# Eight column tiles of a modulation vector made by VectorE in one stage instead of by TensorE in a later one

## The chip, the cores and the metric

One core of a Trainium2 chip runs the whole program. The metric is the device time of one execution in microseconds (us). Below, PE or TensorE is the matrix engine, DVE the vector engine, ACT or ScalarE the activation engine, POOL or GpSimd the fourth compute engine, and SP an engine that here only issues DMAs.

## What is computed

The model has two layers. Each layer has a mixer (input projection, four branches, gated sum, output projection) and a feed-forward (SwiGLU), both with adaptive normalisation. The three groups of 128 tokens (one of a prompt, two of a sample) share all weights. The scale, shift and gate vectors of the normalisation, called modulation, come from a small product with 2 condition vectors, one for each token kind:

```python
def modulation(c_vec, w_mod, b_mod):
    m = (jax.nn.silu(c_vec) @ w_mod + b_mod)[:, None, :]
    return jnp.split(m, 6, axis=-1)
...
for l in range(DEPTH):
    sh_m, sc_m, gt_m, sh_f, sc_f, gt_f = modulation(c, w_mod[l], b_mod[l])
    x, _ = mixer_sublayer(x, sh_m, sc_m, gt_m, p, ctx)
    x = ffn_sublayer(x, sh_f, sc_f, gt_f, p)

def ffn_sublayer(x, shift, scale, gate, p):
    h = rms_norm(x, p['norm_ffn_pre']) * (1.0 + scale) + shift
    f = (jax.nn.silu(h @ p['ffn_w_gate']) * (h @ p['ffn_w_up'])) @ p['ffn_w_down']
    return x + gate * rms_norm(f, p['norm_ffn_post'])
```

A layer's modulation has 6 x 1024 = 6144 columns, 48 tiles of 128. Tiles 32 to 39 (columns 4096 to 5119) are `sc_f`, the scale of the feed-forward's normalisation; it is needed when that layer's mixer has ended.

## The kernel before

All activations are kept transposed, features on the partitions and the 384 tokens along the free axis. Every large weight is split by the kernel into a high and a low part: ACT copies a piece of the raw weight to `whi` (line 419), DVE or POOL subtracts it from the raw weight to give `wlo_` (line 421), and TensorE runs three products per 128 x 128 block (lines 686 to 688: high by high, high by low, low by high). A piece is 512 columns, that is four blocks or 12 products. `take_half` hands out a piece and has the pieces up to four ahead split, into four buffers of each kind (`HB = 4`). Which engine subtracts follows a count: `cnt["n"] % 4 < cnt["pool"]` sends it to POOL. `POOL_FFN = (3, 2)` makes that three of four pieces in the first feed-forward and two of four in the second.

Raw weights come in units of up to 1024 columns, in the order of a list (`layer_plan`), into three buffers. In the mixers ACT's queue issues them, in the feed-forwards SP's. The order of instructions on each engine is fixed when the program is built.

Modulation is made in two ways. In the mixers, `mod_step` follows a gate product (tiles 0 to 23 of 32 in each mixer): it takes one raw unit of `w_mod`, 128 rows by 1024 columns, and multiplies it with the condition vectors on TensorE (`mod_mm`, line 517, four 256-column products). After eight steps ACT copies the sum out (`mod_copy`), TensorE transposes it and DVE adds the bias (`mod_place`, lines 551 and 555). Each step also ends with a `yield`, at which `run` lets the two side programs of the mixer (the recurrent branch and the attention branches) move on; so the steps also set how those are interleaved.

In the feed-forwards, `mod_some` makes whole tiles of 128 output columns on DVE: for each tile a transposed 128 x 1024 weight `rawm` is loaded by SP (three buffers), and `mod_vector` runs two multiply-and-sum instructions on it, one for each condition vector (line 563). `VMOD` lists these tiles and `VMOD_IN` says which feed-forward makes them: 24 in the first, 8 in the second. `add_bias` adds the bias after each eight.

The feed-forward's first part is a loop over tiles m of 128 hidden columns. In each turn TensorE makes gate and up (two pieces each), and `hidden` combines them: ACT line 1763, DVE lines 1764 and 1765, ACT line 1767 (the high part), DVE line 1768 (the low part). Then `mod_some` works on the tiles loaded a turn earlier and issues the loads of the next. Here a turn is called a period; one with two tiles of modulation is a double. The second part multiplies with `ffn_w_down`.

Of the kernel before, what the change touches and what calls it, by code (L numbers as in the profile page):

```python
# [45 lines left out]
HOLD, HLAST = 2, 4  # L46
REST = (5, 6, 7, 7)

VMOD = [(0, m) for m in range(40, 48)] + [(1, m) for m in range(16)] + [(1, m) for m in range(40, 48)]
VMOD_IN = (range(0, 24), range(24, 32))  # L50
YORD = (0, 1, 2, 3, 5, 4, 6, 7)

Z_ORDER = ("vb", "k0", "r0", "va", "k1", "r1", "gq0", "gq1", "gk", "glo")
# [29 lines left out]
def _split_k(nk, width):  # L83
    per = max(1, 1024 // width)
    return [(k, min(per, nk - k)) for k in range(0, nk, per)]


def layer_plan(l):
    out = []

    def gemm(kind, what, nk, width):
        for k, n in _split_k(nk, width):
            out.append((kind, l, what, k, n, width))

    def z(name):
        gemm("z", name, KD, len(COLS[name]))

    def mod(ll, sg, i):
        out.append(("mod", ll, (sg, i // 8), i % 8, 1, 1024))

    for k in KORD:
        out.append(("wide_z", l, None, k, 1, 768))
    for n in Z_ORDER:
        z(n)
    tiles = [(b, m) for b in GATE_ORDER for m in range(8)]
    for i in range(len(tiles) + LAG):
        if i == 8:
            for n in ("cq0", "cq1", "ckv"):
                z(n)
        if i < len(tiles):  # L110
            z("gate%d_%d" % tiles[i])
            if i < 24:
                mod(l, 1 + i // 16, i % 16)
        if i >= LAG:
            b, m = tiles[i - LAG]
            if m % 2 == 1:
                out.append(("br", l, (b, m // 2), 0, 2, 256))
    for m in range(8):
        gemm("out", m, KD, 128)
    for k in KORD:  # L120
        out.append(("wide_f", l, None, k, 1, 768))
    for m in range(3, FM):
        gemm("gate", m, KD, 128)
        gemm("up", m, KD, 128)
    for m in range(8):
        gemm("down", m, FM, 128)
    return out
# [200 lines left out]
def build(tc, I, O):  # L328
# [191 lines left out]
    mod_late = []  # L520
# [259 lines left out]
    def mixer(l, x, xspill, hs, M, merged_of):  # L780
# [67 lines left out]
        def main():  # L848
            for n, q in zip(WIDE_Z, wide_ps):
                z_evac(n)(q)  # L850
            for n in Z_ORDER:
                if n in ("va", "vb"):
                    yield from gemm_tok(("z", l, n), hz, len(COLS[n]), va_evac if n == "va" else vb_evac)
                else:
                    yield from gemm(("z", l, n), hz, z_evac(n))
            tiles = [(b, m) for b in GATE_ORDER for m in range(8)]
            merged = None
            for i in range(len(tiles) + LAG):
                if i == 8:
                    for n in ("cq0", "cq1", "ckv"):  # L860
                        yield from gemm(("z", l, n), hz, z_evac(n))
                if i < len(tiles):
                    b, m = tiles[i]
                    yield from gemm(("z", l, "gate%d_%d" % (b, m)), hz, gate_evac(b, m))
                    if i < 24:
                        mod_step(l, 1 + i // 16, i % 16)
                        yield
                if i == 25 and mod_late:
                    mod_place(*mod_late.pop(), bk_mm())
                if i >= LAG and (i - LAG) % 2:  # L870
                    b, m1 = tiles[i - LAG]
                    yield lambda: b in ready
                    if merged is None:
                        merged = merged_of()
                        mref.append(merged)
                    hi, lo = take_half(next_unit(("br", l, (b, m1 // 2))))[0]
                    for m in (m1 - 1, m1):
                        ps = bk_mm()
                        for k in range(2):
                            o = (m % 2) * 256 + k * 128  # L880
                            xh, xl = brs[b, k][:, 0, :], brs[b, k][:, 1, :]
                            T.matmul(ps[:, :NT], hi[:, o:o + 128], xh, start=(k == 0), stop=False)  # L882
                            T.matmul(ps[:, :NT], hi[:, o:o + 128], xl, start=False, stop=False)  # L883
                            T.matmul(ps[:, :NT], lo[:, o:o + 128], xh, start=False, stop=(k == 1))  # L884
                            yield
                        gt = gates.pop((b, m))
                        if b == GATE_ORDER[0]:
                            V.scalar_tensor_tensor(merged[:, m, :], gt, 1.0, ps[:, :NT], op0=OP.add, op1=OP.mult)
                        else:
                            V.scalar_tensor_tensor(gt, gt, 1.0, ps[:, :NT], op0=OP.add, op1=OP.mult)  # L890
                            (G if m % 2 else V).tensor_add(merged[:, m, :], merged[:, m, :], gt)  # L891
                    if m1 == 7:
                        ready.add(("used", b))
# [814 lines left out]
    for l in range(L):  # L1708
# [18 lines left out]
        with tc.tile_pool(name=f"ffn{l}", bufs=1) as M:  # L1727
            if l + 1 < L:
                load_params(l + 1)
                scale_params(l + 1)  # L1730
                load_rest(l + 1)
            cb = M.tile([128, 2, D], F32, name="cb")
            dma(cb, bass.AP(tensor=csd.tensor, offset=csd.offset, ap=[[0, 128], [D, 2], [1, D]]))
            acc = M.tile([128, len(VMOD), 2], F32, name="acc")
            todo = list(VMOD_IN[l])

            def add_bias(t):

                (ml, m0), t0 = VMOD[t - 7], t - 7
                b = PAR[ml]["vec"][:, V_BMOD + m0:V_BMOD + m0 + 8, None]  # L1740
                V.tensor_add(mod_tile(ml)[:, m0:m0 + 8, :], acc[:, t0:t + 1, :], b.to_broadcast([128, 8, 2]))

            there = []

            def mod_some(n, behind):

                with tc.issue_after(behind.ins):
                    for t, raw in there:
                        junk = M.tile([128, D], F32, name="junk", tag="junk")
                        mod_vector(t, cb, acc, raw, junk)  # L1750
                        if t % 8 == 7:
                            add_bias(t)
                there.clear()
                for t in todo[:n]:
                    raw = M.tile([128, D], F32, name="rawm", tag="rawm", bufs=3)
                    dma(raw, I["wm1"][t])
                    there.append((t, raw))
                del todo[:n]
            hid = []

            def hidden(m, pg, pu):
                th = M.tile([128, NT], F32, name="th", tag="th", bufs=2)
                S.activation(th, pg[:, :NT], AF.Tanh, scale=0.5)
                V.scalar_tensor_tensor(th, th, 1.0, pg[:, :NT], op0=OP.add, op1=OP.mult)
                V.scalar_tensor_tensor(th, th, 0.5, pu[:, :NT], op0=OP.mult, op1=OP.mult)  # L1765
                h = M.tile([128, 2, NT], F32R, name=f"hid{m}", tag=f"hid{m}")
                S.activation(h[:, 0, :], th, AF.Copy)  # L1767
                last = V.tensor_sub(h[:, 1, :], th, h[:, 0, :].bitcast(F32))  # L1768
                hid.append((h[:, 0, :], h[:, 1, :]))
                return last  # L1770

            def ffn_main():
                got = list(wide_ps)
                cnt["pool"] = POOL_FFN[l]
                for m in range(3):
                    hidden(m, got[2 * m], got[2 * m + 1])
                hk = [hs[k] for k in range(KD)]
                for m in range(3, FM):
                    got = []
                    bk = (bk_at, bk_mm)[m % 2]  # L1780
                    yield from gemm(("gate", l, m), hk, got.append, bk=bk)
                    yield from gemm(("up", l, m), hk, got.append, bk=bk)
                    ins = hidden(m, *got)
                    mod_some(2 if m % 3 == 0 else 1, ins)

            drive(ffn_main())
            assert not todo and not there
            cnt["pool"] = POOL_FFN[l] - 1 if l == 0 else 1
            last = l + 1 == L
            mg, ps = out_gemm("down", l, hid, post_scale(l, 1), x, M, "z", ("sq0", "sq1", "sq2"), ("th",), not last)  # L1790
            if last:
                post_norm(x, mg, ps[0])
            else:
                hs, sx = bridge(x, mg, ps, sx, scales(l + 1, 0), shift(l + 1, 0), ("wide_z", l + 1, None))
# [27 lines left out]
```

## Time and profile before

| what | value |
|---|---|
| time, median of 3 runs | 1599.79 us (1592.71 to 1599.82) |
| the profiled execution | 1595.09 us, of which the traced span is 1593.3 us |
| PE busy | 1539.9 us (97%) |
| DVE busy | 973.9 us (61%) |
| ACT busy | 640.0 us (40%) |
| POOL busy | 460.7 us (29%) |
| line 517 in the two mixers | 384 records, 391 ns each |
| line 563 | 64 instructions, 1460 ns each |

Shares are averages over the span. A matmul counts as busy from its start to its modelled end, so consecutive ones overlap: two starts, not two durations, give the pace. One f32 matmul of line 517 shows as two records.

### The profile page before, as it was taken

The numbers are of one execution on the slowest core, as the hardware profiler recorded it, in microseconds if no ns is written. First come the engines' busy times: TensorE is split into PE (matmuls) and PEld (weight loads), VectorE is DVE, ScalarE is ACT, GpSimd is POOL, SyncE is SP. The second block draws the span as 40 slices with busy tenths as digits, with TensorE's granted clock in tenths as the row PEclk, the third lists the DMA queues.
The fourth block names the chain that finished last, engine by engine and source line by source line (L and its number), as shares of the span: only waits on it lengthen the run. The fifth ranks groups of instructions, "written<-read, shape, count | busy, mean of one in ns | idle before, by whom it ended". The sixth has DMA issues, their size and how long they took to land. (4 is left out here: it accounts for less than half of the span.)

```text
span 1593.3 us, 28472 instructions
## 1 busy us (share of the span) xinstructions
PE 1539.9 (97%) x11036; PEld 1394.9 (88%) x11036; DVE 973.9 (61%) x2165; ACT 640.0 (40%) x1364; POOL 460.7 (29%) x357
## 2 busy tenths in 40 slices
PE   8999999999999999999989999999999989999997
PEld 6988778777899999999989887876789889999997
DVE  5478458844558677863475774677554777844333
ACT  3454334432343544433345533434323435444331
POOL 2210002111226555544452100012012453433222
PEclk9999999999998999999999999999999989999999
DMA  8544343435542556644334542353354416544332
GB/s 330 196 130 136 97 130 110 137 94 150 165 159 77 188 197 213 213 154 130 113 110 130 150 132 79 110 144 110 95 156 131 160 54 213 181 132 130 119 125 77
DMA packets 106759, 225.32 MB, mean 141 GB/s; under 512 B 41280, under 2 KB 51584, under 8 KB 105728
## 3 DMA queue, kind: packets, MB, share of 16 engines
q1 hardware_dynamic: 76384, 124.99, 24.9%
q10 hardware_dynamic: 30240, 98.51, 19.3%
q8 instruction: 87, 1.43, 0.4%
q14 instruction: 48, 0.39, 0.1%
HBM read 214.38 MB, written 9.08 MB: 140 GB/s over the span
## 5 line engine op out<-in xcount | busy, mean ns | idle before, releaser
L419 ACT ACTIVATE whi<-raw 128x512 fp32r<-128x512 f32 (+2 forms) x580 | 345.9, 603 | 492.0 <-PE bank L687 265.2
L686 PE MATMUL bank<-hk,whi 128*128 128x384 f32 x1424 | 501.2, 352 | 1.5 <-DVE gate L890 0.9
L687 PE MATMUL bank<-hk,whi 128*128 128x384 f32 x1424 | 481.0, 338 | 1.9 <-DVE hk L1527 1.9
L686 PEld LDWEIGHTS bank<-hk,whi 128*128 128x128 f32 x1424 | 268.1, 188 | 26.7 <-issue 14.6
L687 PEld LDWEIGHTS bank<-hk,whi 128*128 128x128 f32 x1424 | 268.4, 188 | 6.6 <-DVE hk L1527 3.1
L686 PE MATMUL bank<-hid,whi 128*128 128x384 f32 x352 | 119.1, 338 | 0.0
L687 PE MATMUL bank<-hid,whi 128*128 128x384 f32 x352 | 118.9, 338 | 0.0
L563 DVE SCALAR_TENSOR_TENSOR junk<-rawm,cb 128x1024 f32<-128x1024 f32 x64 | 93.4, 1460 | 0.5
L710 PE MATMUL bank<-hk,whi 128*128 128x384 f32 x192 | 62.9, 341 | 6.1 <-DVE hk L618 5.6
L708 PE MATMUL bank<-hk,whi 128*128 128x384 f32 x192 | 65.5, 341 | 0.9 <-ACT hk L610 0.7
L687 PEld LDWEIGHTS bank<-hid,whi 128*128 128x128 f32 x352 | 66.1, 188 | 0.0
L686 PEld LDWEIGHTS bank<-hid,whi 128*128 128x128 f32 x352 | 66.1, 188 | 0.0
L891 POOL TENSOR_TENSOR merged<-merged,gate 128x384 f32<-128x384 f32 x24 | 29.3, 1221 | 111.8 <-DVE gate L890 98.4
L1564 POOL TENSOR_TENSOR acc<-acc,sqo 128x384 f32<-128x384 f32 x42 | 51.3, 1233 | 30.9 <-ACT sqo L1554 15.8
L1768 DVE TENSOR_TENSOR hid<-th,hid 128x384 fp32r<-128x384 f32 x44 | 42.7, 970 | 22.6 <-ACT hid L1767 22.6
L843 ACT ACTIVATE gate<-bank 128x384 f32<-128x384 f32 x64 | 31.1, 486 | 61.4 <-PE bank L688 49.9
L1765 DVE SCALAR_TENSOR_TENSOR th<-th,bank 128x384 f32<-128x384 f32 x44 | 24.3, 552 | 37.9 <-PE bank L688 37.4
L911 ACT ACTIVATE prob<-bank,tiny 128x384 f32<-128x384 f32 (+1 forms) x56 | 27.2, 485 | 47.5 <-DVE tiny L910 40.2
L1557 DVE TENSOR_SCALAR mg<-bank,Q 128x128 f32<-128x128 f32 x64 | 23.6, 408 | 32.7 <-ACT sqo L1554 31.5
L710 PEld LDWEIGHTS bank<-hk,whi 128*128 128x128 f32 x192 | 35.8, 188 | 8.4 <-DVE hk L618 6.6
L890 DVE SCALAR_TENSOR_TENSOR gate<-gate,bank 128x384 f32<-128x384 f32 x48 | 26.4, 550 | 22.1 <-PE bank L884 21.8
L708 PEld LDWEIGHTS bank<-hk,whi 128*128 128x128 f32 x192 | 36.5, 190 | 2.2 <-ACT hk L610 1.1
(2019 smaller groups left out, 3581.2 us busy)
## 6 DMA issues: line engine op xcount, KB each, us to landing
raw<-in_w ACTq DMA_DIRECT2D x150, 512.0 KB, 3.6
raw<-in_w SPq DMA_DIRECT2D x108, 512.0 KB, 3.5
rawm<-in_wm SPq DMA_DIRECT2D x32, 512.0 KB, 3.5
raw<-in_w SPq DMA_DIRECT2D x41, 384.0 KB, 3.0
wm<-in_wm SPq DMA_DIRECT2D x16, 512.0 KB, 7.6
raw<-in_w ACTq DMA_DIRECT2D x32, 256.0 KB, 2.6
raw<-in_w ACTq DMA_DIRECT2D x15, 384.0 KB, 3.6
bt<-in_bt SPq DMA_DIRECT2D x8, 256.0 KB, 4.2
```

Source lines behind the costliest of these rows:

```text
L419: last_split[:] = [S.activation(hi[:, :w], raws[i][:, sl], AF.Copy)]
L563: V.scalar_tensor_tensor(junk, raw, 1.0, cb[:, g, :], op0=OP.mult, op1=OP.mult, accum_out=acc[:, t, g:g + 1])
L686: T.matmul(ps[:, :n], wh, xh, start=(k == 0), stop=False)
L687: T.matmul(ps[:, :n], wh, xl, start=False, stop=False)
L708: T.matmul(o, wh, xh, start=(i == 0), stop=False)
L710: T.matmul(o, wh, xl, start=False, stop=(i == 7))
L843: S.activation(gates[b, m], ps[:, :NT], AF.Tanh, scale=0.5)
L890: V.scalar_tensor_tensor(gt, gt, 1.0, ps[:, :NT], op0=OP.add, op1=OP.mult)
L891: (G if m % 2 else V).tensor_add(merged[:, m, :], merged[:, m, :], gt)
L911: S.activation(e[:, :n], src, AF.Exp, bias=nb, scale=scale, accum_out=sm)
L1564: (V if i == 1 else G).tensor_add(a, a, b)
L1768: last = V.tensor_sub(h[:, 1, :], th, h[:, 0, :].bitcast(F32))
```

## The change

The eight steps of layer 1 that made tiles 32 to 39 leave the second mixer, and the eight tiles join the list of the first feed-forward, which makes 32 tiles now. The loads move with them: eight raw units of 512 KB leave ACT's queue in the second mixer, eight `rawm` loads of 512 KB join SP's queue in the first feed-forward. `mod_some` takes two tiles in every period instead of two, one, one; that also holds for the eight tiles of the second feed-forward.

```diff
--- before.py
+++ after.py
@@ -46,8 +46,9 @@
 HOLD, HLAST = 2, 4
 REST = (5, 6, 7, 7)
 
-VMOD = [(0, m) for m in range(40, 48)] + [(1, m) for m in range(16)] + [(1, m) for m in range(40, 48)]
-VMOD_IN = (range(0, 24), range(24, 32))
+VMOD = [(0, m) for m in range(40, 48)] + [(1, m) for m in (*range(16), *range(32, 40))] + [(1, m) for m in range(40, 48)]
+VMOD_IN = (range(0, 32), range(32, 40))
+MMOD = (24, 16)
 YORD = (0, 1, 2, 3, 5, 4, 6, 7)
 
 Z_ORDER = ("vb", "k0", "r0", "va", "k1", "r1", "gq0", "gq1", "gk", "glo")
@@ -109,7 +110,7 @@
                 z(n)
         if i < len(tiles):
             z("gate%d_%d" % tiles[i])
-            if i < 24:
+            if i < MMOD[l]:
                 mod(l, 1 + i // 16, i % 16)
         if i >= LAG:
             b, m = tiles[i - LAG]
@@ -862,10 +863,10 @@
                 if i < len(tiles):
                     b, m = tiles[i]
                     yield from gemm(("z", l, "gate%d_%d" % (b, m)), hz, gate_evac(b, m))
-                    if i < 24:
+                    if i < MMOD[l]:
                         mod_step(l, 1 + i // 16, i % 16)
                         yield
-                if i == 25 and mod_late:
+                if i == MMOD[l] + 1 and mod_late:
                     mod_place(*mod_late.pop(), bk_mm())
                 if i >= LAG and (i - LAG) % 2:
                     b, m1 = tiles[i - LAG]
@@ -1781,7 +1782,7 @@
                     yield from gemm(("gate", l, m), hk, got.append, bk=bk)
                     yield from gemm(("up", l, m), hk, got.append, bk=bk)
                     ins = hidden(m, *got)
-                    mod_some(2 if m % 3 == 0 else 1, ins)
+                    mod_some(2, ins)
 
             drive(ffn_main())
             assert not todo and not there
```

Line numbers in the changed kernel are one higher than before. On DVE, in the middle of the first feed-forward (`hid` is the hidden tile's low part, `th` its two steps, `junk` the modulation, `wlo_` a weight's low part), the program before reads, from one period's end over a double into a single:

```order
L1768 TENSOR_TENSOR hid_6831<-th,hid_6831 128x384
L563 SCALAR_TENSOR_TENSOR junk,acc<-rawm,cb 128x1024
L421 TENSOR_TENSOR wlo__6862<-raw,whi 128x512
L563 SCALAR_TENSOR_TENSOR junk,acc<-rawm,cb 128x1024 x2
L1764 SCALAR_TENSOR_TENSOR th<-th,bank 128x384
L563 SCALAR_TENSOR_TENSOR junk,acc<-rawm,cb 128x1024
L1765 SCALAR_TENSOR_TENSOR th<-th,bank 128x384
L1768 TENSOR_TENSOR hid_6916<-th,hid_6916 128x384
L563 SCALAR_TENSOR_TENSOR junk,acc<-rawm,cb 128x1024
L421 TENSOR_TENSOR wlo__6944<-raw,whi 128x512
L563 SCALAR_TENSOR_TENSOR junk,acc<-rawm,cb 128x1024
L1764 SCALAR_TENSOR_TENSOR th<-th,bank 128x384
```

The same place in the changed program, two periods:

```order
L1769 TENSOR_TENSOR hid_6764<-th,hid_6764 128x384
L564 SCALAR_TENSOR_TENSOR junk,acc<-rawm,cb 128x1024
L422 TENSOR_TENSOR wlo__6797<-raw,whi 128x512
L564 SCALAR_TENSOR_TENSOR junk,acc<-rawm,cb 128x1024 x2
L1765 SCALAR_TENSOR_TENSOR th<-th,bank 128x384
L564 SCALAR_TENSOR_TENSOR junk,acc<-rawm,cb 128x1024
L1766 SCALAR_TENSOR_TENSOR th<-th,bank 128x384
L1769 TENSOR_TENSOR hid_6851<-th,hid_6851 128x384
L564 SCALAR_TENSOR_TENSOR junk,acc<-rawm,cb 128x1024
L422 TENSOR_TENSOR wlo__6884<-raw,whi 128x512
L564 SCALAR_TENSOR_TENSOR junk,acc<-rawm,cb 128x1024 x2
L1765 SCALAR_TENSOR_TENSOR th<-th,bank 128x384
```

Every period is now a double: four modulation instructions stand between one `hid` and the next, three of them ahead of the first `th` step, and none of the periods has only two.

On DVE in the second feed-forward, where two weight pieces of four are DVE's, the program before reads, for its second and third period with modulation, one tile each:

```order
L1768 TENSOR_TENSOR hid_14741<-th,hid_14741 128x384
L563 SCALAR_TENSOR_TENSOR junk,acc<-rawm,cb 128x1024 x2
L421 TENSOR_TENSOR wlo__14786<-raw,whi 128x512
L1764 SCALAR_TENSOR_TENSOR th<-th,bank 128x384
L421 TENSOR_TENSOR wlo__14804<-raw,whi 128x512
L1765 SCALAR_TENSOR_TENSOR th<-th,bank 128x384
L1768 TENSOR_TENSOR hid_14823<-th,hid_14823 128x384
L563 SCALAR_TENSOR_TENSOR junk,acc<-rawm,cb 128x1024 x2
L421 TENSOR_TENSOR wlo__14870<-raw,whi 128x512
L1764 SCALAR_TENSOR_TENSOR th<-th,bank 128x384
```

and in the changed program:

```order
L1769 TENSOR_TENSOR hid_14729<-th,hid_14729 128x384
L564 SCALAR_TENSOR_TENSOR junk,acc<-rawm,cb 128x1024 x3
L422 TENSOR_TENSOR wlo__14779<-raw,whi 128x512
L564 SCALAR_TENSOR_TENSOR junk,acc<-rawm,cb 128x1024
L422 TENSOR_TENSOR wlo__14797<-raw,whi 128x512
L1765 SCALAR_TENSOR_TENSOR th<-th,bank 128x384
L1766 SCALAR_TENSOR_TENSOR th<-th,bank 128x384
L1769 TENSOR_TENSOR hid_14816<-th,hid_14816 128x384
L564 SCALAR_TENSOR_TENSOR junk,acc<-rawm,cb 128x1024 x3
L422 TENSOR_TENSOR wlo__14866<-raw,whi 128x512
L564 SCALAR_TENSOR_TENSOR junk,acc<-rawm,cb 128x1024
L422 TENSOR_TENSOR wlo__14884<-raw,whi 128x512
```

The doubles stand next to each other now, with both low parts behind the third and the fourth modulation instruction.

On TensorE in the second mixer, at one of the eight steps (`hk` is the normalised input, `brX` a branch's output), the program before reads:

```order
L687 MATMUL bank<-hk,whi 128x384
L688 MATMUL bank<-hk,wlo__12830 128x384
L517 MATMUL bank<-raw,cs 32x256 x4
L882 MATMUL bank<-brX,whi 128x384
L883 MATMUL bank<-brX,whi 128x384
L884 MATMUL bank<-brX,wlo__12910 128x384
```

and now:

```order
L688 MATMUL bank<-hk,whi 128x384
L689 MATMUL bank<-hk,wlo__12841 128x384
L883 MATMUL bank<-brX,whi 128x384
L884 MATMUL bank<-brX,whi 128x384
L885 MATMUL bank<-brX,wlo__12883 128x384
```

The step is gone and the branch product follows the gate product directly. Elsewhere between the steps the side programs' matmuls stand a few rows from where they stood.

## Rows read from the trace of the kernel before

**Rows 1.** All engines by windows, first feed-forward; busy PE PEld DVE ACT POOL, clock, DMA.

```profile
560.00:600.00 40.00, 40.00 (x232) 40.00 (x231) 31.97 (x48) 16.76 (x30) 22.46 (x14) 1.00 0.60 203
```

**Rows 2.** TensorE's timeline, second mixer: start, duration, line, operation; x8 are eight records.

```profile
1182.41 0.34 PE L688 MATMUL bank<-hk,wlo__13022 128*128 128x384 f32 x1
1182.68 0.64 PE L517 MATMUL bank<-raw,cs 128*32 128x256 f32 x8
1183.25 0.45 PE L882 MATMUL bank<-brX,whi 128*128 128x384 f32 x1
```

**Rows 3.** TensorE's timeline at the placing of the removed columns, second mixer.

```profile
1207.54 0.34 PE L688 MATMUL bank<-hk,wlo__13279 128*128 128x384 f32 x1
...
1208.37 0.44 PE L882 MATMUL bank<-brX,whi 128*128 128x384 f32 x1 [0.27 <-DVE MOD L555]
```

**Rows 4.** DVE's timeline, first feed-forward, a period with two tiles and the next.

```profile
610.09 0.55 DVE L1765 SCALAR_TENSOR_TENSOR th<-th,bank 128x384 f32<-128x384 f32 x1 [1.26 <-PE bank L688]
...
612.32 1.21 DVE L563 SCALAR_TENSOR_TENSOR junk<-rawm,cb 128x1024 f32<-128x1024 f32 x1
...
615.32 2.21 DVE L563 SCALAR_TENSOR_TENSOR junk<-rawm,cb 128x1024 f32<-128x1024 f32 x1
...
617.92 1.85 DVE L563 SCALAR_TENSOR_TENSOR junk<-rawm,cb 128x1024 f32<-128x1024 f32 x1
...
619.71 0.54 DVE L1765 SCALAR_TENSOR_TENSOR th<-th,bank 128x384 f32<-128x384 f32 x1
620.84 0.56 DVE L1768 TENSOR_TENSOR hid<-th,hid 128x384 fp32r<-128x384 f32 x1 [0.59 <-ACT hid L1767]
621.32 1.22 DVE L563 SCALAR_TENSOR_TENSOR junk<-rawm,cb 128x1024 f32<-128x1024 f32 x1
...
622.46 0.69 DVE L421 TENSOR_TENSOR wlo__6944<-raw,whi 128x512 fp32r<-128x512 f32 x1
...
626.73 0.56 DVE L1765 SCALAR_TENSOR_TENSOR th<-th,bank 128x384 f32<-128x384 f32 x1 [1.97 <-PE bank L688]
```

**Rows 5.** POOL's timeline in the same stretch.

```profile
608.59 1.30 POOL L421 TENSOR_TENSOR wlo__6812<-raw,whi 128x512 fp32r<-128x512 f32 x1 [0.47 <-ACT whi L419]
...
614.84 1.60 POOL L421 TENSOR_TENSOR wlo__6879<-raw,whi 128x512 fp32r<-128x512 f32 x1 [2.87 <-ACT whi L419]
...
619.00 1.94 POOL L421 TENSOR_TENSOR wlo__6926<-raw,whi 128x512 fp32r<-128x512 f32 x1 [0.31 <-ACT whi L419]
```

**Rows 6.** POOL's and DVE's timelines in the first output product.

```profile
478.41 1.07 POOL L1564 TENSOR_TENSOR acc<-acc,sqo 128x384 f32<-128x384 f32 x1 [2.89 <-ACT sqo L1560]
...
478.52 1.50 DVE L421 TENSOR_TENSOR wlo__5497<-raw,whi 128x512 fp32r<-128x512 f32 x1
```

**Rows 7.** TensorE's timeline: first use of two low parts that DVE made.

```profile
618.55 0.33 PE L688 MATMUL bank<-hk,wlo__6862 128*128 128x384 f32 x1
...
626.87 0.33 PE L688 MATMUL bank<-hk,wlo__6944 128*128 128x384 f32 x1
```

**Rows 8.** ScalarE's timeline, first feed-forward: the hidden tile's copy and the split behind it.

```profile
620.28 0.53 ACT L1767 ACTIVATE hid<-th 128x384 fp32r<-128x384 f32 x1 [1.36 <-DVE th L1765]
620.71 0.62 ACT L419 ACTIVATE whi<-raw 128x512 fp32r<-128x512 f32 x1
```

**Rows 9.** DVE's timeline, second feed-forward, a period with two tiles.

```profile
1344.64 0.56 DVE L1765 SCALAR_TENSOR_TENSOR th<-th,bank 128x384 f32<-128x384 f32 x1 [0.85 <-PE bank L688]
...
1351.54 0.69 DVE L421 TENSOR_TENSOR wlo__14704<-raw,whi 128x512 fp32r<-128x512 f32 x1
...
1354.54 0.55 DVE L1765 SCALAR_TENSOR_TENSOR th<-th,bank 128x384 f32<-128x384 f32 x1
```

**Rows 10.** TensorE's timeline there: first use of that low part.

```profile
1355.19 0.33 PE L688 MATMUL bank<-hk,wlo__14704 128*128 128x384 f32 x1
```

**Rows 11.** All engines by windows, two bridges; clock is the number behind POOL's.

```profile
520.00:525.00 5.00, 2.46 (x13) 1.82 (x12) 5.00 (x9) 2.24 (x5) 3.38 (x3) 1.00 0.28 79
...
805.00:810.00 5.00, 3.77 (x16) 3.80 (x17) 4.17 (x13) 1.75 (x4) 1.47 (x3) 0.52 0.00 0
```

## The prediction

> **What bounds the kernel now.** I read the busy shares first, then the windows of the two stages that the change touches, then the timelines of each engine there. In the first feed-forward TensorE is busy for all 40 us of a window while DVE is busy for 31.97 and POOL for 22.46 [rows 1], so by the shares TensorE sets the pace and DVE has a fifth to spare. The pace itself is the distance between the first uses of two low parts that stand at the same place of neighbouring periods: 626.87 - 618.55 = 8.32 us [rows 7]. That is 48 products at 0.173 us, without a gap.
>
> The timelines show why DVE's share misleads. A modulation instruction takes 1.21 us when POOL is idle, but 2.21 us and 1.85 us where POOL has asked during the one before it [rows 4, 5]. POOL's subtraction is longer too in those places, 1.60 and 1.94 us instead of 1.30 [rows 5]. So the two take turns: whoever has asked first works, the other stands still and still counts as busy. It needs no pause on DVE: in another stage POOL asked at 478.41, and DVE's next subtraction, from 478.52, took 1.50 us [rows 6] instead of 0.69 [rows 4]. The `th` steps, which read one operand from PSUM, take 0.54 to 0.56 us wherever they stand [rows 4]. The resource to count is therefore DVE's instructions with two SBUF operands plus POOL's, together.
>
> In a double (the period with two tiles) DVE already falls behind. Line 1765 should start 8.32 us after 610.09, at 618.41, and starts at 619.71, 1.30 us late. In the single behind it DVE waits 1.97 us for TensorE at 626.73 [rows 4]: it has caught up.
>
> **What the change removes.** One step in the second mixer: the last product before it starts at 1182.41, the next one behind it at 1183.25 [rows 2]. Without the step that would be 0.17 later, so it costs 0.84 - 0.17 = 0.67 us of TensorE, and eight cost 5.4. Placing the result costs 1208.37 - 1207.54 - 0.17 = 0.66 us, with DVE's bias addition waited for [rows 3]. Together -6.0 us, all on TensorE, which has hardly a gap there. The side programs' instructions move by a few rows at the same time; I take that at nothing. Its bounds: such a move could end or make a wait, and the nearest rows with one are the 1.97 and 1.26 of [rows 4]; so 2 us either way.
>
> **What it adds in the first feed-forward.** Eight tiles are 16 modulation instructions, and all 16 periods with modulation are doubles now. What does a double cost when the next is a double too? From 612.32, the first instruction behind `hid`, to 621.32, the same one a period later, DVE took 9.00 us. In it are 2.21 - 1.21 = 1.00 and 1.85 - 1.21 = 0.64 of standing still for POOL [rows 4], so its own work, with ScalarE's 0.59 inside, is 7.36. POOL has three subtractions in each period (by the count rule, three pieces of four), and each can hold DVE up by 1.00. A double behind a double thus takes between 9.00 (as in the row, where POOL's third fell beside `th` and the wait for ScalarE) and 7.36 + 3 x 1.00 = 10.36. Over TensorE's 8.32 that is an excess of 0.68 to 2.04; the row of line 1765 gave 1.30.
>
> I take 1.30 for the first three doubles and 2.04 for the other 13, for this reason. When line 1765 is late, ScalarE's copy in line 1767 is late, and the splits stand behind it in ScalarE's order: at 620.28 the copy had waited 1.36 us for DVE, and the split came directly behind [rows 8]. What POOL subtracts are these splits. Once DVE is late for good, POOL's three requests come in a bunch behind the copy, where DVE runs `hid`, modulation, split, modulation, modulation, all of them with two SBUF operands, and not beside `th`.
>
> How much lateness is hidden? DVE's own low part of each period was done at 622.46 + 0.69 = 623.15, with DVE 1.30 late, and TensorE first used it at 626.87 [rows 4, 7]: 3.7 us of reserve. So TensorE stands still when DVE is 1.3 + 3.7 = 5.0 late. The sum of the excesses is 3 x 1.30 + 13 x 2.04 = 30.4; less 5.0 that is 25.4 us of standing TensorE. By the bounds: 1.3 + 15 x 0.68 - 5.0 = 6.5, and 1.3 + 15 x 2.04 - 5.0 = 26.9.
>
> The Trainium skill (SBUF — State Buffer, section Who interferes with whom) calls the DVE and GpSimd port pair an exclusive lock that is held for the whole instruction, and says a DVE instruction with two SBUF inputs contends with a GpSimd one that reads SBUF. The rows agree on the turns, but the hold-up was 1.00 us and not the 1.30 of an undisturbed POOL subtraction. By the rule the stage would lose 37 us instead of 25 (rival 3); the measured hold-up decides for me.
>
> The loads: eight times 512 KB more on SP, over some 130 us, which is 32 GB/s beside 203 GB/s at a share of 0.60 [rows 1]; hidden, and by proportion the share becomes 0.70. A `rawm` load waits on SP for the modulation of an earlier tile to free its buffer, and the raw weights' loads are queued behind it. With DVE late these are late too, but a raw unit has three buffers and the split needs it later than the low part that I counted, so I give it no price of its own. If that cover were gone, TensorE would wait a load's time on top, once a period; this is in the upper end.
>
> **The second feed-forward.** The same eight tiles come in four doubles running, not two doubles among four singles. Two pieces of four are DVE's here, so a double's own work is 7.36 + 0.61 = 7.97 (a split of 0.69 overlaps its neighbour by 0.08), with POOL's two 9.97, an excess of 1.65. The first double is 9.90 - 8.32 = 1.58 late [rows 9]. The earlier low part was done at 1352.23 and used at 1355.19, 2.96 us of reserve [rows 9, 10]. In the third double it comes some 3.2 late and in the fourth 4.9: TensorE loses about 2 us, between 0 and 3.
>
> **Sum.** On the profiled execution: 1595.1 - 6.0 + 25.4 + 2 = 1616.5. That execution lies 4.7 below the median of the runs shown (1599.8) and 2.4 above the fastest (1592.7), so on the median's scale it is 1621.2. I take the middle, 1619.
>
> **Rivals.** (1) POOL's subtractions keep falling beside `th` and the wait for ScalarE. Then the excess is 0.68, as in [rows 4], up to the 1.30 of line 1765. The stage loses 6.5 to 15.8, and the whole changes by 0 to +12: 1598 to 1610, middle 1604. For it: it is what a double does today. Against it: today's double starts from a DVE in time. Chance 0.17.
>
> (2) The other side, not slower: the reserve of 5.0 us hides it all. It decides at an excess of 5.0 / 16 = 0.31 per double. Then only the 6.0 saved remains: 1593 on the middle scale. For it: DVE is busy for only 31.97 of 40, and TensorE never stands today. Against it: even the mildest excess that the rows give is twice that. Chance 0.10.
>
> (3) More than the forecast: TensorE's standing takes its clock down. A bridge window had TensorE busy for 2.46 of 5 us at a granted clock of 1.00, another 3.77 of 5 at 0.52, the lower of its two levels (1.2 and 2.4 GHz) [rows 11], so short standing alone did not lower it, and 2 us in 10 should not. If it did for 3 us in each of 13 periods, it would add some 20: 1639. Or POOL holds DVE up for the whole 1.30 us of an undisturbed subtraction [rows 5]: the late double takes 7.36 + 3.90 = 11.26, the stage loses 3 x 1.30 + 13 x 2.94 - 5.0 = 37, and the time is 1631; the 1.00 of [rows 4] speaks against it. Chance of the two 0.10. The second is what the Trainium skill's rule, above, would do here.
>
> (4) The change doesn't give the mixer's saving, since a wait of the side programs takes its place: +6, 1625. Chance 0.05.
>
> **Chances and range.** The forecast has 0.58; its own range is 1611 to 1627 (excess of a late double 1.7 to 2.3, the scale between profile and median). 0.5% is 8 us, about what a measurement of this kernel tells from no change. Slower by more: the forecast, (3), (4) and a quarter of (1), 0.77. Within: three quarters of (1) and half of (2), 0.18. Faster by more: half of (2), since 6 us with the runs' spread may pass 8, 0.05. The range 1601 to 1632 leaves out (2), the lower part of (1) and the worst of (3).
>
> **What would show it.** Right: in the first feed-forward periods of 10.2 to 10.6 us from about the fifth double on, TensorE waiting once a period for a DVE-made `wlo_`, line 1767 waiting several us for line 1765, and modulation instructions near 2.2 us twice or thrice in a period; two periods without modulation at the end back at 8.32. In the second mixer 64 fewer records of line 517's kind and some 6 us less. Wrong: periods of 8.32 throughout (then the reserve was larger), periods near 9.0 (then POOL's turns stay hidden), a clock below 1.00 in this stage, or a longer mixer.

## The result

The changed kernel takes 1617.99 us (median of 4 runs, 1614.74 to 1620.19), the kernel before 1596.25 (4 runs, 1592.19 to 1599.82). The ratio is 1.0135 with a 95% interval of 1.0108 to 1.0161: slower by 1.4%, some 22 us. The forecast was 1619, in a range of 1601 to 1632.

The profiled execution took 1618.09 us. From its page, the span, the busy time of each engine, and the group of the modulation instructions (busy us, mean ns, idle time before):

```profile
span 1616.3 us, 28394 instructions
...
PE 1542.1 (95%) x10970; PEld 1396.4 (86%) x10970; DVE 1020.7 (63%) x2197; ACT 634.5 (39%) x1363; POOL 476.0 (29%) x357
...
L564 DVE SCALAR_TENSOR_TENSOR junk<-rawm,cb 128x1024 f32<-128x1024 f32 x80 | 134.3, 1679 | 0.8
```

TensorE has nearly the same busy time (1542.1 against 1539.9 us) over a span that is 23 us longer. The 16 more modulation instructions cost DVE not 16 x 1.46 = 23 us but 41 (93.4 to 134.3): the mean of all went from 1460 ns to 1679. Of the 64 in the first feed-forward 29 took 2.1 us or more; before the change it was 6 of 48.

The windows of the first feed-forward (busy time of PE, PEld, DVE, ACT, POOL, then clock and DMA), the first to be held against [rows 1]:

```profile
560.00:600.00 40.00, 40.00 (x232) 39.86 (x231) 37.24 (x51) 13.33 (x25) 24.59 (x13) 1.00 0.60 199
...
640.00:680.00 40.00, 35.15 (x189) 33.87 (x188) 37.50 (x46) 12.15 (x24) 21.54 (x12) 0.96 0.58 202
...
720.00:760.00 40.00, 38.33 (x220) 37.80 (x219) 20.35 (x31) 14.27 (x27) 17.27 (x13) 1.00 0.40 124
```

DVE went from 31.97 to 37.24 and then to 37.50 of 40, and TensorE from 40.00 to 35.15; in the last window, in which modulation ends at 726.6, DVE is down to 20.35.

Landmarks of the two profiled executions give the stages: the first `tanh` of each feed-forward (line 1763 before), and the broadcasts of the sums at the end of each stage (line 498 before).

| stretch | before, us | after, us | difference |
|---|---|---|---|
| start to the end of the first mixer | 509.08 | 506.96 | -2.1 |
| bridge to the first feed-forward's first `tanh` | 31.92 | 33.33 | +1.4 |
| gate and up part, first `tanh` to last | 156.87 | 188.74 | +31.9 |
| rest of the first feed-forward | 104.20 | 100.50 | -3.7 |
| second mixer, to the end of its output product | 491.91 | 485.19 | -6.7 |
| second feed-forward | 288.95 | 291.20 | +2.3 |

The first two rows hold the same work in both kernels, so their -0.7 is scatter. The first feed-forward lost 28.2 us, the second 2.3, and the mixer won 6.7.

What the lost time is made of stands in DVE's timeline, a period from one `hid` (line 1769 now) to the next, to be held against [rows 4]:

```profile
642.83 0.56 DVE L1769 TENSOR_TENSOR hid<-th,hid 128x384 fp32r<-128x384 f32 x1 [0.59 <-ACT hid L1768]
643.30 1.22 DVE L564 SCALAR_TENSOR_TENSOR junk<-rawm,cb 128x1024 f32<-128x1024 f32 x1
...
644.45 1.78 DVE L422 TENSOR_TENSOR wlo__7060<-raw,whi 128x512 fp32r<-128x512 f32 x1
646.16 2.32 DVE L564 SCALAR_TENSOR_TENSOR junk<-rawm,cb 128x1024 f32<-128x1024 f32 x1
...
648.52 2.21 DVE L564 SCALAR_TENSOR_TENSOR junk<-rawm,cb 128x1024 f32<-128x1024 f32 x1
...
651.12 1.21 DVE L564 SCALAR_TENSOR_TENSOR junk<-rawm,cb 128x1024 f32<-128x1024 f32 x1
...
652.27 0.55 DVE L1766 SCALAR_TENSOR_TENSOR th<-th,bank 128x384 f32<-128x384 f32 x1
653.40 0.56 DVE L1769 TENSOR_TENSOR hid<-th,hid 128x384 fp32r<-128x384 f32 x1 [0.59 <-ACT hid L1768]
653.88 1.22 DVE L564 SCALAR_TENSOR_TENSOR junk<-rawm,cb 128x1024 f32<-128x1024 f32 x1
```

From 643.30 to 653.88 a period takes 10.58 us. The second modulation instruction takes 2.32 us and the third 2.21, the first and the fourth 1.22 and 1.21, and the split's low part 1.78 instead of 0.69: three hold-ups. They answer to POOL's three subtractions of the period, which now come back to back, as [rows 5] doesn't show them:

```profile
643.91 1.77 POOL L422 TENSOR_TENSOR wlo__7077<-raw,whi 128x512 fp32r<-128x512 f32 x1 [5.05 <-ACT whi L420]
645.65 1.74 POOL L422 TENSOR_TENSOR wlo__7095<-raw,whi 128x512 fp32r<-128x512 f32 x1
647.36 2.29 POOL L422 TENSOR_TENSOR wlo__7129<-raw,whi 128x512 fp32r<-128x512 f32 x1
```

They come together because ScalarE had to wait for DVE first:

```profile
642.27 0.53 ACT L1768 ACTIVATE hid<-th 128x384 fp32r<-128x384 f32 x1 [7.39 <-DVE th L1766]
642.70 1.14 ACT L420 ACTIVATE whi<-raw 128x512 fp32r<-128x512 f32 x2
```

ScalarE waited 7.39 us for the second `th` step, and the splits that feed POOL stand right behind that copy; in [rows 8] it was 1.36. So POOL's three turns meet DVE's run of instructions with two SBUF operands, and while DVE is at `th` and waits for ScalarE, POOL has nothing to do.

On TensorE it looks like this, the first, the second, the eighth and the last of twelve waits for a low part that DVE makes, and one behind them:

```profile
603.86 0.44 PE L689 MATMUL bank<-hk,wlo__6710 128*128 128x384 f32 x1 [2.29 <-DVE wlo__6710 L422]
...
614.40 0.44 PE L689 MATMUL bank<-hk,wlo__6797 128*128 128x384 f32 x1 [1.95 <-DVE wlo__6797 L422]
...
677.95 0.44 PE L689 MATMUL bank<-hk,wlo__7322 128*128 128x384 f32 x1 [1.95 <-DVE wlo__7322 L422]
...
720.58 0.44 PE L689 MATMUL bank<-hk,wlo__7667 128*128 128x384 f32 x1 [0.37 <-DVE wlo__7667 L422]
...
730.15 0.44 PE L687 MATMUL bank<-hid,whi 128*128 128x384 f32 x1 [1.30 <-DVE th L1765]
```

From the first to the last of these uses are 116.72 us for 11 periods, 10.61 each, where [rows 7] had 8.32.

### The profile page after: what moved, and what is told of

Same layout as the page of the kernel before. It is cut to its first block, busy times and chain, and to the rows that moved or that the text cites. A ratio compares the mean times of both kernels' runs of the same rounds, so it can differ in the third digit from the quotient of the medians.

```text
span 1616.3 us, 28394 instructions
## 1 busy us (share of the span) xinstructions
PE 1542.1 (95%) x10970; PEld 1396.4 (86%) x10970; DVE 1020.7 (63%) x2197; ACT 634.5 (39%) x1363; POOL 476.0 (29%) x357
## 5 line engine op out<-in xcount | busy, mean ns | idle before, releaser
L564 DVE SCALAR_TENSOR_TENSOR junk<-rawm,cb 128x1024 f32<-128x1024 f32 x80 | 134.3, 1679 | 0.8
L1768 ACT ACTIVATE hid<-th 128x384 fp32r<-128x384 f32 x44 | 23.1, 525 | 123.8 <-DVE th L1766 122.7
L1769 DVE TENSOR_TENSOR hid<-th,hid 128x384 fp32r<-128x384 f32 x44 | 34.0, 773 | 22.5 <-ACT hid L1768 22.5
```

The lines of the kernel that those rows point to most:

```text
L564: V.scalar_tensor_tensor(junk, raw, 1.0, cb[:, g, :], op0=OP.mult, op1=OP.mult, accum_out=acc[:, t, g:g + 1])
```

## The experiments

The edits are to the changed kernel, unless the kernel before is named. Ratios are to the kernel before.

**e1: no turns.** All low parts of the first gate and up part on DVE, none on POOL:

```diff
-                cnt["pool"] = POOL_FFN[l]
+                cnt["pool"] = 0 if l == 0 else POOL_FFN[l]
```

> The changed kernel, but in the first feed-forward's gate and up part all low parts are subtracted by DVE, none by POOL. Theory (DVE and POOL take turns at a shared port, and POOL's three turns make the late period 10.5 us): DVE's own work becomes 7.36 + 3 x 0.61 = 9.2 us and nothing holds it up, so periods are near 9.2 though DVE has more to do; the stage loses some 16 x 0.87 - 5 = 9 us instead of 28, and the time is near 1600. Modulation instructions take 1.21 us each. Rival (DVE is simply too full, its long instructions are its own): three more subtractions per period make it 10.55 + 1.8 = 12.4 us, and the time near 1645.

Measured: 1587.57 us, ratio 0.9932 (0.9909 to 0.9955). More work for DVE, and some 30 us less than the changed kernel. The window of all engines:

```profile
600.00:640.00 40.00, 40.00 (x232) 40.00 (x231) 40.00 (x72) 16.57 (x30) 0.00 (x0) 1.00 0.76 249
```

DVE is busy for the whole window, POOL not at all, and TensorE never waits. DVE's timeline, a period from the modulation behind one `hid` to the next (subtractions of 0.69 between):

```profile
643.77 1.23 DVE L564 SCALAR_TENSOR_TENSOR junk<-rawm,cb 128x1024 f32<-128x1024 f32 x1
...
644.92 0.69 DVE L422 TENSOR_TENSOR wlo__7251<-raw,whi 128x512 fp32r<-128x512 f32 x1
...
648.88 1.23 DVE L564 SCALAR_TENSOR_TENSOR junk<-rawm,cb 128x1024 f32<-128x1024 f32 x1
...
650.49 0.69 DVE L422 TENSOR_TENSOR wlo__7304<-raw,whi 128x512 fp32r<-128x512 f32 x1
651.09 0.69 DVE L422 TENSOR_TENSOR wlo__7322<-raw,whi 128x512 fp32r<-128x512 f32 x1
651.69 0.56 DVE L1769 TENSOR_TENSOR hid<-th,hid 128x384 fp32r<-128x384 f32 x1
652.16 1.23 DVE L564 SCALAR_TENSOR_TENSOR junk<-rawm,cb 128x1024 f32<-128x1024 f32 x1
```

Each modulation instruction here takes 1.22 or 1.23 us, and none of the stage's 64 took as much as 1.3. A period takes 652.16 - 643.77 = 8.39 us and not the 9.2 that I had put together: the two low parts at 650.49 and 651.09 stand between `th` and `hid` and fill the wait for ScalarE, 0.59 of the 0.8, which I had counted beside them. 8.39 is so close to TensorE's 8.32 that the lateness of 16 doubles stays in the reserve. The rival, a DVE that is too full by itself, is out.

**e2 and e10: one and two low parts of four on POOL.** The same line with 1 and with 2.

> As e1, but one of four low parts stays with POOL. Theory of turns: 7.36 + 2 x 0.61 + 1.07 = 9.65 us per late period, a loss of 16 x 1.33 - 5 = 16 us, time near 1606, between e1 and the changed kernel. Rival (DVE too full by itself): 10.55 + 1.2 = 11.8 us, time near 1637.

> The changed kernel with two of four low parts on POOL in the first gate and up part: the point between the changed kernel (three, periods of 10.55) and e2 (one, 9.09). Theory of turns: about 1.07 - 0.61 = 0.5 us less per period than with three, and the wait for ScalarE partly filled as in e2: periods of 9.7 to 10.1 us, time near 1608. Rival (DVE too full by itself): longer than 10.55.

Measured: with one 1598.93 us (ratio 1.0009, 0.9994 to 1.0025), with two 1607.33 in a single run. TensorE's waits for DVE's low part, two periods of each, first with one on POOL, then with two:

```profile
623.05 0.44 PE L689 MATMUL bank<-hk,wlo__6919 128*128 128x384 f32 x1 [0.18 <-DVE wlo__6919 L422]
...
632.14 0.44 PE L689 MATMUL bank<-hk,wlo__7008 128*128 128x384 f32 x1 [0.16 <-DVE wlo__7008 L422]
```

```profile
617.73 0.44 PE L689 MATMUL bank<-hk,wlo__6884 128*128 128x384 f32 x1 [0.98 <-DVE wlo__6884 L422]
...
627.30 0.45 PE L689 MATMUL bank<-hk,wlo__6973 128*128 128x384 f32 x1 [0.96 <-DVE wlo__6973 L422]
```

The periods are 9.09 and 9.57 us, so the series for none, one, two and three subtractions on POOL is 8.32 (TensorE's pace), 9.09, 9.57 and 10.58: fewer instructions on DVE, longer periods. I had expected 9.65 for one and 9.7 to 10.1 for two: both are too high, probably because here too I had counted ScalarE's wait beside low parts that fill it (e1).

**e3: the adding half alone.** The mixer keeps its eight steps:

```diff
-MMOD = (24, 16)
+MMOD = (24, 24)
```

> Only the adding half of the change: the first feed-forward makes the eight tiles too, and the second mixer keeps its eight steps and makes them again. Theory: the feed-forwards lose as in the changed kernel (+28 and +2) and nothing is won in the mixer: about 6 us above the changed kernel, 1624 to 1626. Rival (the mixer's saving was not real, the stages only shifted): the same time as the changed kernel, 1618.

Measured: 1625.86 us, ratio 1.0171 (1.0144 to 1.0198), by the medians 7.9 over the changed kernel, by the ratios 5.7, with intervals that overlap. The second mixer took 496.05 us in e3's profile against 485.19. Both point to a real saving in the mixer; what shows it is e5, below.

**e4: the second feed-forward at its old pace.**

```diff
-                    mod_some(2, ins)
+                    mod_some(2 if l == 0 or m % 3 == 0 else 1, ins)
```

> The changed kernel with the second feed-forward's tiles at the old pace of two, one, one. Theory: four doubles in a row cost that stage its 2.2 us, so it is 2 us under the changed kernel, about 1616, with the second feed-forward as long as before. Rival (that stage's difference is scatter between executions): no difference.

Measured: 1613.63 us, ratio 1.0100 (1.0076 to 1.0124), by the medians 4.4 under the changed kernel, with intervals that overlap. The stage itself is the better witness: 287.92 us in e4's profile against 291.20. The changed kernel has two waits there that e4 and the kernel before don't have, in the third and the fourth double:

```profile
1394.17 0.44 PE L689 MATMUL bank<-hk,wlo__14866 128*128 128x384 f32 x1 [1.04 <-DVE wlo__14866 L422]
...
1404.43 0.44 PE L689 MATMUL bank<-hk,wlo__14950 128*128 128x384 f32 x1 [1.58 <-DVE wlo__14950 L422]
```

**e5: the removing half alone.** The list, its ranges and the pace as before, with the shorter mixer (`MMOD`, the plan and the mixer's loop as in the change); the tiles' place is filled with another eight tiles:

```diff
-VMOD = [(0, m) for m in range(40, 48)] + [(1, m) for m in (*range(16), *range(32, 40))] + [(1, m) for m in range(40, 48)]
-VMOD_IN = (range(0, 32), range(32, 40))
+VMOD = [(0, m) for m in range(40, 48)] + [(1, m) for m in range(16)] + [(1, m) for m in range(40, 48)]
+VMOD_IN = (range(0, 24), range(24, 32))
...
+                if (ml, m0) == (1, 8):
+                    V.tensor_add(mod_tile(ml)[:, 32:40, :], acc[:, t0:t + 1, :], b.to_broadcast([128, 8, 2]))
...
-                    mod_some(2, ins)
+                    mod_some(2 if m % 3 == 0 else 1, ins)
```

> Only the removing half of the change: the second mixer drops its eight steps and nobody makes the eight tiles (their place gets a copy of another eight, so the output is wrong); feed-forwards as before. Theory: the 6.0 us of the removed work, so a ratio of 0.996 to the kernel before, about 1591, and a second mixer some 6 us shorter. Rival (a wait of the side programs takes the place of the removed work): ratio 1.000.

Measured: 1591.93 us, ratio 0.9970 (0.9952 to 0.9988), 4.8 us less, by its interval 1.9 to 7.7; the 6.0 lie inside.

**e6: the tiles in the stage's second part.** The old pace in the gate and up part, and one tile behind each of the first output tiles of the down product (a new argument `after` of `out_gemm`):

```diff
+            if after:
+                after(end[0])
...
-                    mod_some(2, ins)
+                    mod_some(2 if m % 3 == 0 else 1, ins)
...
-            mg, ps = out_gemm("down", l, hid, post_scale(l, 1), x, M, "z", ("sq0", "sq1", "sq2"), ("th",), not last)
+            mg, ps = out_gemm("down", l, hid, post_scale(l, 1), x, M, "z", ("sq0", "sq1", "sq2"), ("th",), not last, (lambda ins: mod_some(1, ins)) if l == 0 else None)
```

> The eight tiles made by DVE in the first feed-forward's second part (one in each of the first output tiles), the gate and up part and the second feed-forward at the old pace of two, one, one. Theory: in the second part DVE is busy for some 17 of 40 us and POOL for 20, a period there is 11.4 us long, so a tile's 2.4 us plus two turns of 1.07 fit, TensorE doesn't wait, and the 6.0 us of the mixer remain: ratio 0.996, as e5. Rival (any eight tiles more in that stage cost as much as they did): ratio near 1.01.

Measured: 1588.66 us, ratio 0.9949 (0.9931 to 0.9968). A window of the down product:

```profile
720.00:760.00 40.00, 40.00 (x233) 40.00 (x232) 26.12 (x41) 15.39 (x28) 22.05 (x17) 1.00 0.60 193
```

DVE 26.12 and POOL 22.05 of 40, TensorE without a gap: the same eight tiles cost TensorE nothing here.

**e7: e1 with the second feed-forward's old pace** (the lines of e1 and e4 together).

> e1 (all low parts on DVE in the first gate and up part) with the second feed-forward at the old pace. Theory: e1's 1587 less the 2.2 us that four doubles in a row cost: ratio 0.992, about 1585. Rival: as e1, 0.993 to 0.994, not to be told apart in time but in the length of the second feed-forward.

Measured: 1585.24 us, ratio 0.9932 (0.9913 to 0.9950), the fastest median of all, some 11 us under the kernel before. Its ratio is e1's, so the two can't be told apart in time; the second feed-forward took 287.93 us, in e1 291.17.

**e8: control, the kernel before with e1's line.**

> Control: the kernel before, with all low parts on DVE in the first gate and up part. Theory: TensorE never waited in that stage, so taking the turns away wins nothing: ratio 1.000. Rival (e1 was faster because of the subtractions on DVE themselves, not because they stop the lateness): ratio 0.997 or less.

Measured: 1595.95 us, ratio 0.9994 (0.9981 to 1.0007). Where no lateness reaches TensorE, taking the turns away wins nothing.

**e9: the kernel before in another rhythm.** The same 24 tiles, six doubles first and twelve singles behind them:

```diff
-                    mod_some(2 if m % 3 == 0 else 1, ins)
+                    mod_some((2 if m < 9 else 1) if l == 0 else 2 if m % 3 == 0 else 1, ins)
```

> The kernel before with its 24 tiles in another rhythm: the first six periods are doubles, the other twelve singles (before: two, one, one all along). Same instructions, same loads. Theory (lateness adds up over doubles in a row, the first five microseconds of it are hidden): 3 x 1.30 + 3 x 2.2 - 5.0 = 5.5 us of standing TensorE in the fifth and sixth period, time 4 to 6 us over before, ratio 1.003. Rival (it is the amount of work in the stage that counts): ratio 1.000 and no wait of TensorE in the stage.

Measured: 1603.34 us, ratio 1.0043 (1.0026 to 1.0061), about 7 us more for the same instructions. TensorE's waits in the gate and up part, all there are, between the use of a DVE-made low part a period ahead and the one behind:

```profile
592.17 0.42 PE L688 MATMUL bank<-hk,wlo__6623 128*128 128x384 f32 x1
...
603.12 0.44 PE L688 MATMUL bank<-hk,wlo__6710 128*128 128x384 f32 x1 [2.27 <-DVE wlo__6710 L421]
...
613.65 0.44 PE L688 MATMUL bank<-hk,wlo__6795 128*128 128x384 f32 x1 [1.92 <-DVE wlo__6795 L421]
...
624.22 0.44 PE L688 MATMUL bank<-hk,wlo__6877 128*128 128x384 f32 x1 [1.97 <-DVE wlo__6877 L421]
...
634.23 0.33 PE L688 MATMUL bank<-hk,wlo__6959 128*128 128x384 f32 x1
```

They begin where they began in the changed kernel (603.86), after four doubles in a row, and the gate and up part took 165.64 us instead of 156.87, 8.8 more. The rest of the stage was as long as before (104.20). The four periods shown took 10.95, 10.53, 10.57 and 10.01 us, together 8.8 over four of 8.32; the fourth has no wait, and its 1.7 us are the clock's (last section). I had expected 5.5, in two periods. It is the order of the doubles that costs, not the amount of work.

## Why the prediction was right, step by step

**The bound.** That TensorE sets the pace only while DVE and POOL together keep up, with the turns as the limit, is shown by e1, e2, e10 and e8: work moved from POOL to DVE shortened the period where DVE was late, and did nothing for the time where TensorE did not wait. In e8, as in e1, no modulation instruction of the stage took as much as 1.3 us.

**The mixer's -6.0.** Measured -6.7 between the two profiles, 4.8 in e5 (with its interval) and 5.7 between e3 and the changed kernel by their ratios. What I could not see from one trace is how much this stage scatters: in the profiles of this study it took 491.9 to 501.2 us with the eight steps (four kernels) and 482.7 to 491.7 without (eight kernels). The means differ by 10. The scatter goes with the granted clock; the longest stage (e9, with the steps) and the shortest (e7, without):

```profile
809.42:1310.61 501.19, 482.82 (x3716) 411.50 (x3716) 312.02 (x784) 203.19 (x468) 107.52 (x87) 0.96 0.41 122
```

```profile
799.68:1282.40 482.72, 466.84 (x3649) 402.86 (x3650) 307.82 (x782) 203.69 (x467) 109.28 (x87) 0.99 0.39 118
```

As an estimate, multiply each of the twelve lengths by its granted clock, unrounded: the gate and up part of e9 (last section) lost to a low clock just what this takes off. That leaves 483.0 to 485.3 us with the steps and 474.8 to 481.3 without. The means, 483.9 and 477.4, are 6.5 apart, near the 6.0; the other 3.7 go with the clock, and whether the removed steps had a part in that is not shown. Nor is it shown why e1 and e7 win, by their ratios, some 11 us in all: e7's interval, 8 to 14, leaves out the 6.0.

**The late double.** Put together from one double in time, the late one was to take 10.36 us, and it took 10.58 between modulations of one place; the choice of three full turns against the row's 9.00 was right, and the reason given, ScalarE's copy ahead of POOL's splits, is what the traces show (7.39 us of waiting, three subtractions back to back). Most of the missing 0.22 is the size of a turn: the three hold-ups were 1.09, 1.10 and 0.99 us, together 3.18, where 3.00 had been taken. That it would not happen with another order on ScalarE was not tried.

**The reserve.** Here two errors nearly cancel, which is luck. The prediction added the 1.30 us that line 1765 was late to the 3.7 that it had read; but the low part itself was only 0.7 late there. In a period of the kernel before with DVE in time the low part was done at 613.46 + 0.68 = 614.14 and used at 618.55 [rows 7], a reserve of 4.4 and not 5.0:

```profile
613.46 0.68 DVE L421 TENSOR_TENSOR wlo__6862<-raw,whi 128x512 fp32r<-128x512 f32 x1
```

The first three doubles were milder than taken, too: in the changed kernel they took 9.02, 9.02 and 10.14 us between modulations of one place, an excess of 3.2 in all and not of 3 x 1.30. So TensorE's first wait comes behind the fourth double, as reckoned, in the changed kernel, in e4 and in e9.

**The stage's +25.4.** Measured +28.2. The term that was a little small is the excess, 2.04 for a late double: it was 2.26 between modulations of one place (10.58 - 8.32), or 2.29 over the eleven periods between TensorE's twelve waits (10.61 - 8.32). The gate and up part even lost 31.9, of which 3.7 came back in the rest of the stage: the last `tanh` stood on ScalarE behind a copy that had waited 7.15 us for DVE, while TensorE had gone on. The last lateness also cost a wait of 1.30 us at 730.15, at the start of the down product, which the prediction had not named; it had expected the two periods at the end back at TensorE's pace.

**The second feed-forward's +2.** Measured +2.3, and 3.2 to 3.3 against the kernels with the old pace (the changed kernel against e4, e1 against e7). The waits are in the third and the fourth double as forecast (1.04 and 1.58 us); the third was larger than forecast, 3.2 of lateness less 2.96 of reserve.

**The rivals.** The mild excess (1) and the hidden one (2) did not come. Of (3), the clock did fall, but in the changed kernel's late periods it cost nothing (below); that it would not fall, since TensorE stands for only 2 us in 10, was wrong, and "a clock below 1.00 in this stage", which the prediction had set as a sign of being wrong, came true (0.96 in the window from 640). The other half of (3), hold-ups of 1.30 us, is out: they were 0.99 to 1.10, and the period 10.58 and not 11.26. (4) is out by e5.

**The total.** That 1619 lies within about 1 us of the measured time is partly luck. The terms were off by -0.7, +2.8 and +0.3, and the choice of a middle between the profile's scale and the median's was alone worth some 2 us either way.

## What to carry to other kernels

Count DVE's instructions with two SBUF operands and POOL's instructions as one resource, DVE's by their undisturbed durations and POOL's by the hold-up that one causes (0.99 to 1.10 us in the period shown), before using a share of idle DVE time: here a DVE that was busy for 31.97 of 40 us, by the count, could not take eight tiles more at no cost. When DVE runs late, taking work off POOL and giving it to DVE can be the remedy: the same change with POOL's subtractions on DVE is 0.7% faster than the kernel before (e1), and with the tiles in the next stage, where DVE and POOL have room, it is 0.5% faster (e6). And let heavy periods alternate with light ones: six heavy ones in a row cost 7 us that the same work in the rhythm two, one, one did not.

## What the runs showed that I had not expected

In the stage where TensorE waited 2 us in 10.5, its granted clock fell, and the periods did not change. Windows of 2 us in the changed kernel, around the wait at 614.40 (the number behind POOL's is the clock):

```profile
612.00:614.00 2.00, 0.45 (x3) 0.13 (x1) 2.00 (x3) 1.39 (x3) 1.94 (x2) 1.00 1.00 379
...
616.00:618.00 2.00, 2.00 (x8) 2.00 (x7) 1.97 (x3) 0.00 (x0) 1.74 (x1) 0.50 0.16 43
618.00:620.00 2.00, 2.00 (x9) 2.00 (x9) 2.00 (x4) 0.00 (x0) 0.00 (x0) 0.67 0.92 340
...
620.00:622.00 2.00, 2.00 (x13) 2.00 (x12) 1.41 (x5) 1.06 (x3) 0.00 (x0) 1.00 0.62 197
```

And TensorE's next wait for a low part, from its timeline:

```profile
624.97 0.45 PE L689 MATMUL bank<-hk,wlo__6884 128*128 128x384 f32 x1 [0.38 <-DVE wlo__6884 L422]
```

Behind the wait the clock went to 0.50, the lower of its two levels (1.2 of 2.4 GHz), and it was back at 1.00 in the window from 620. TensorE then arrived later at the next low part and waited only 0.38 us there instead of 1.95, and the period was as long as the others: DVE set it. This happened behind four of the stage's eight waits of 1.9 us or more, and each time the next wait was 0.37 to 0.58; behind the other four, as that of 2.29 us at 603.86, the clock stayed at 1.00, and what decides is not shown. In e10, with waits of about 1 us, the clock of the stage stayed at 1.00, and so it did in e1, without waits.

Where DVE no longer sets the pace, the low clock does cost time. In e9 the last of the three waits ends at 624.22, with single periods behind it:

```profile
624.00:626.00 2.00, 1.78 (x9) 1.78 (x10) 2.00 (x2) 0.00 (x0) 2.00 (x2) 0.93 0.05 20
626.00:628.00 2.00, 2.00 (x8) 2.00 (x8) 1.44 (x4) 0.42 (x1) 1.58 (x1) 0.50 0.25 53
628.00:630.00 2.00, 2.00 (x10) 2.00 (x9) 1.86 (x4) 0.82 (x3) 0.00 (x0) 0.72 0.96 338
```

The clock that is missing in these windows, 0.07, 0.50 and 0.28 of 2 us each, makes 1.70 us, and the next period, to 634.23, took 10.01 us instead of 8.32, 1.69 more. So while DVE sets the pace, neither the clock nor the length of TensorE's waits tells what the stage loses; the distance between two uses of the same place does.
